# A wide second expert product and a rebuilt router stage in a two-block transformer kernel on one Trainium2 core

## The chip, the core and the metric

The kernel runs on one NeuronCore of one Trainium2 chip. The metric is device microseconds of one execution, taken as the median of several runs. The times of the single instructions come from one further execution under the hardware profiler.

## What is computed

Two transformer blocks run over 2048 tokens of width 1024 in fp32. The first is a hybrid mixer, the second has two kinds of attention and a layer of 32 experts. The change touches the end of the second block: the attention output is projected, added to the residual and normalised (h1); a router picks four experts per token; each expert is a gated MLP; the gated sums are added and normalised again.

```python
h = _layernorm(DEEPNORM_ALPHA_2 * h + mix, ln1_g[i], ln1_b[i])
...
def _moe_sequence(h, w_router, b_router, w_gate_up, b_gate_up, w_down, b_down):
    L = h.shape[0]
    logits = (jnp.einsum('ld,de->le', h, w_router) + b_router).astype(jnp.float32)
    top_val, top_idx = lax.top_k(logits, TOP_K)
    gates = jax.nn.softmax(top_val, axis=-1).astype(h.dtype)
    ...
    hgu = lax.ragged_dot(xs, w_gate_up, group_sizes) + b_gate_up[e_sorted]
    act = _clamped_swiglu(hgu)
    out = lax.ragged_dot(act, w_down, group_sizes) + b_down[e_sorted]
    out = out * gates.reshape(-1)[order][:, None]
    return jax.ops.segment_sum(out, tok, num_segments=L)
```

## The kernel before

Every fp32 product is made of three TensorE products of a high and a low part (`mm3`, lines 72 to 74): a weight or activation is cast on ScalarE to the high part (line 67), and the rest is taken by a subtraction on VectorE or GpSimd (line 68). The engines have their own instruction queues and each works strictly in the order in which the program issues; the program writes that order out by hand.

**The router stage** (`phase_f`, about 2532 to 2824 us) runs over 16 tiles of 128 tokens. `project(n)` multiplies tile n by the output weights: two column halves, eight steps of three products of 512 columns each, and after each half VectorE adds the residual (line 1579). While tile n is projected, a `plan` (lines 1855 to 1862) places the other work of its neighbours at steps 0 to 15: `normed(n-1)` at the start (row statistics, line 1586 and 1588, then a reciprocal square root in two GpSimd instructions, lines 78 and 79), `finished(n-1)` (ScalarE normalises, VectorE multiplies by the gain, GpSimd adds the bias, then SyncE stores h1), the router product and `select(n-2)` (scores, the four best, their exponentials, the one-hot rows `hot` and their sum `mk`), `share` (the gates), `gates` (a dense row of gates), `places` (two small TensorE products of `mk` count the tokens of each expert, VectorE works out each token's slot in its expert's table), four `scatter`s (GpSimd indirect DMAs into four tables), and `bias_t` and `bias` (the experts' output biases, line 1690 transposes the dense gates). After the last projection a tail does what is left: all routing of the last two tiles, the six scatters that were left over and the four of the last tile, the ranking of the experts by load (`ranks`), the last biases and `overflow`. Only then SyncE can read which expert comes first, and the expert stage begins with reading the tables (line 1949) and gathering the token rows (line 1968).

**The expert stage** (`phase_g`, to the end) runs 16 rounds of two experts, A and B, with fixed capacities (`CAPS`). An expert's first product (`up`) has eight items of 256 weight columns, its second (`down`) four. Each item is one 1 MB weight load into `raw` (three buffers) on SyncE, cut into two halves (`split_half`, five buffers of each part) that are made two items ahead (`ensure`). An `up` item makes two PSUM tiles (`pj`, four buffers), which are evicted by `gate`, and one item later `glu` and `keep` write the activation into `at[:, f]` for item f. A `down` item multiplies all eight parts of `at` by 256 columns of the second weights, into a PSUM tile `pd` (two buffers) for each token tile; ScalarE scales it by the gate into `y` (line 2107). In the last round the final sum of all tokens and its normalisation run beside the work (`Finish`); the last expert adds its rows onto the sums, normalises them (`RowNorm`) and stores them by indirect DMA. There an `eager` flag lets the first `down` item of all token tiles run on seven of the eight parts before the eighth is waited for.

Of the kernel before, what the change touches and what calls it, by code (L numbers as in the profile page):

```python
# [20 lines left out]
KD = D // 128  # L21
# [1495 lines left out]
def phase_f(cx, a, op, o, h, h1, acc, tables, out):  # L1517
# [3 lines left out]
    with es, tc.tile_pool(name="fp", bufs=4, space=PSUM) as pj, \  # L1521
# [48 lines left out]
        def project(i):  # L1570
            d = st[i]
            ht = d["ht"]
            for m in range(2):
# [5 lines left out]
                nc.vector.scalar_tensor_tensor(ht[:, ms], ht[:, ms], ALPHA, ps, op0=OP.mult, op1=OP.add)  # L1579

        def normed(i):
            d = st[i]
            ht = d["ht"]
            bs = t_.tile([128, 2, 6], F32, name="bs")
            for m in range(2):
                nc.vector.bn_stats(bs[:, m, :], ht[:, m * 512:(m + 1) * 512])
            mv = t_.tile([128, 4], F32, name="mv")
            nc.vector.bn_aggr(mv[:, 0:2], bs)
            cx.rsqrt(mv[:, 2:3], mv[:, 1:2], LN_EPS, 1)
            nc.vector.tensor_scalar(mv[:, 3:4], mv[:, 0:1], mv[:, 2:3], -1.0, op0=OP.mult, op1=OP.mult)  # L1590
            d["mv"] = mv

        def finished(i):
            d = st[i]
            hn = d["hn"] = t_.tile([128, D], F32, name="hn", bufs=4)
            step = D if i < NT - 1 else 512
# [17 lines left out]
        def select(i):  # L1614
# [11 lines left out]
            nc.scalar.activation(gt, v8[:, :TOPK], AF.Exp, bias=nv, accum_out=gs)  # L1626
            i8 = t_.tile([128, 8], mybir.dt.uint32, name="i8")
# [4 lines left out]
            for k in range(TOPK):  # L1632
                nc.vector.tensor_scalar(hot[:, k, :], iof[:, :NE], idf[:, k:k + 1], None, op0=OP.is_equal)
# [8 lines left out]
        def share(i):  # L1642
            gt, gs = st[i]["gt"], st[i]["gs"]
            nc.vector.reciprocal(gs, gs)
            nc.vector.tensor_scalar(gt, gt, gs, None, op0=OP.mult)

        def gates(i):
            d = st[i]
            gt, hot = d["gt"], d["hot"]
            gm = d["gm"] = t_.tile([128, 3, NE], F32, name="gm")  # L1650
            g1 = t_.tile([128, NE], F32, name="g1")
# [3 lines left out]
            three = [q[:, None, :].to_broadcast([128, 3, NE]) for q in (hot[:, TOPK - 1, :], g1)]  # L1655
            nc.vector.scalar_tensor_tensor(gm, three[0], gt[:, TOPK - 1:TOPK], three[1], op0=OP.mult, op1=OP.add)

        def places(i):
            d = st[i]
            gt, hot = d["gt"], d["hot"]  # L1660
# [5 lines left out]
            nc.vector.tensor_tensor(pos, pos, ebase, OP.add)  # L1666
            nc.vector.tensor_tensor(run, ps[:, NE:2 * NE], run, OP.add)
# [4 lines left out]
            di = t_.tile([128, TOPK], I32, name="di")  # L1672
            nc.vector.tensor_copy(di, dst)
            en = t_.tile([128, TOPK, 2], F32, name="en")
            nc.vector.tensor_copy(en[:, 0, 0:1], ids[:, 0, i:i + 1])
            row = t_.tile([128, TOPK], I32, name="row")
            nc.vector.tensor_scalar(row, di, 127, None, op0=OP.bitwise_and)
            nc.vector.tensor_copy(en[:, :, 1], gt)
            nc.vector.tensor_scalar(en[:, 1:, 0], row[:, 1:], -1.0, ids[:, 1, i:i + 1], op0=OP.mult, op1=OP.add)
            d["di"], d["en"] = di, en  # L1680
# [28 lines left out]
        def ranks(_):  # L1709
            pc = pr.tile([128, 512], F32, name="r")  # L1710
# [810 lines left out]
```

## Time and profile before

| | us |
|---|---|
| median of 3 runs | 5385.56 (5380.69 to 5391.58) |
| the profiled execution | 5383.15 |
| its span, first to last instruction | 5381.2 |

Times in the rows are microseconds from the span's start. A row of a timeline gives start, length, engine, line, operation, the tiles written and read, and in brackets how long the engine had been idle before and what ended that. A TensorE product's length is modelled and overlaps the next one's, so its cost is read from start to start. PEclk is the granted TensorE clock: 1.00 is 2.4 GHz and 0.50 is 1.2 GHz.

### The profile page before, as it was taken

How to read it: one execution, taken by the hardware profiler on the slowest of the kernel's cores; microseconds unless marked ns; L12 is line 12 of the kernel's file. 1: busy time of each engine (PE TensorE's matmuls, PEld its weight loads, DVE VectorE, ACT ScalarE, POOL GpSimd, SP SyncE). 2: the span in 40 equal slices, each digit the busy share in tenths (PEclk: the TensorE clock that was granted, in tenths of full speed). 3: DMA queues.
4: the chain of work that ended last, by engine and by line, in shares of the span. 5: the costliest groups of instructions: out<-in, count | busy, mean ns of one | idle time of the engine just before them, and what ended most of it. 6: DMA issues, size and time to landing. Idle time of an engine off the chain costs nothing. (4 is left out here: it accounts for less than half of the span.)

```text
span 5381.2 us, 89111 instructions
## 1 busy us (share of the span) xinstructions
PE 5179.1 (96%) x33672; PEld 4795.2 (89%) x33672; DVE 3721.3 (69%) x6827; ACT 2690.7 (50%) x5404; POOL 1607.1 (30%) x1571
## 2 busy tenths in 40 slices
PE   8999999899899999999979999999999999999997
PEld 7888878688799999998769999999999999998886
DVE  6787777634688866666887755667767667767758
ACT  4344433333577755555326444545545555556543
POOL 1232226655100021001443233223333333323227
PEclk9999999899999999999989999999999999999998
DMA  4333344344520011011437566556666666767675
GB/s 132 114 106 98 98 143 162 118 125 138 152 67 27 29 52 36 28 36 61 147 103 224 178 182 184 164 163 201 202 195 204 195 202 187 213 188 207 203 212 181
DMA packets 733017, 761.08 MB, mean 141 GB/s; under 512 B 109700, under 2 KB 673870, under 8 KB 732582
## 3 DMA queue, kind: packets, MB, share of 16 engines
q1 hardware_dynamic: 702768, 678.51, 40.3%
q0 software_dynamic: 27776, 74.33, 5.6%
q8 instruction: 267, 4.37, 0.3%
q10 hardware_dynamic: 2038, 2.48, 0.1%
q14 instruction: 168, 1.38, 0.1%
HBM read 626.35 MB, written 128.84 MB: 140 GB/s over the span
## 5 line engine op out<-in xcount | busy, mean ns | idle before, releaser
L68 DVE TENSOR_TENSOR wlo<-raw,whi 128x1024 fp32r<-128x1024 f32 (+1 forms) x751 | 925.8, 1243 | 433.1 <-ACT whi L67 428.5
L67 ACT CAST whi<-raw 128x1024 fp32r<-128x1024 f32 (+1 forms) x1000 | 961.6, 988 | 491.8 <-PE pj L73 176.7
L68 POOL TENSOR_TENSOR wlo<-raw,whi 128x1024 fp32r<-128x1024 f32 (+1 forms) x249 | 553.6, 2223 | 1708.0 <-ACT whi L67 1600.3
L72 PE MATMUL pj<-xsA,whi 128*128 128x256 f32 (+11 forms) x1792 | 595.2, 332 | 20.8 <-DVE g L2048 9.9
L73 PE MATMUL pj<-xsA,whi 128*128 128x256 f32 (+11 forms) x1792 | 592.2, 330 | 0.1
L74 PE MATMUL pj<-xsA,wlo 128*128 128x256 f32 (+11 forms) x1792 | 590.6, 330 | 0.3 <-DVE wlo L68 0.3
L67 ACT CAST ph<-T 128x512 fp32r<-128x512 f32 x512 | 301.0, 588 | 374.8 <-PE T L1349 369.2
L2016 PE MATMUL pj<-xsB,whi 128*128 128x312 f32 (+11 forms) x1664 | 482.2, 360 | 3.9 <-DVE g L2046 3.9
L68 DVE TENSOR_TENSOR pl<-T,ph 128x512 fp32r<-128x512 f32 x512 | 353.4, 691 | 165.5 <-ACT ph L67 156.1
L2018 PE MATMUL pj<-xsB,wlo 128*128 128x156 f32 (+11 forms) x1664 | 417.6, 251 | 0.0
L72 PE MATMUL pd<-whi,atA 128*128 128x256 f32 (+4 forms) x1360 | 395.3, 291 | 17.4 <-ACT atA L67 15.0
L73 PE MATMUL pd<-wlo,atA 128*128 128x256 f32 (+4 forms) x1360 | 384.4, 283 | 8.1 <-POOL wlo L68 7.0
L1330 ACT ACTIVATE P<-S,nm 128x384 f32<-128x384 f32 (+2 forms) x640 | 384.6, 610 | 8.1 <-DVE nm L1324 4.8
L74 PE MATMUL pd<-whi,atA 128*128 128x256 f32 (+4 forms) x1360 | 384.0, 282 | 4.0 <-DVE atA L68 3.9
L72 PEld LDWEIGHTS pj<-xsA,whi 128*128 128x128 f32 x1792 | 341.1, 190 | 35.0 <-ACT g L2043 10.6
L1319 DVE TENSOR_REDUCE mx<-S 128x1 f32<-128x384 f32 (+2 forms) x640 | 355.1, 580 | 24.5 <-PE S L1318 21.5
L74 PEld LDWEIGHTS pj<-xsA,wlo 128*128 128x128 f32 x1792 | 341.4, 191 | 11.3 <-DVE wlo L68 0.5
L73 PEld LDWEIGHTS pj<-xsA,whi 128*128 128x128 f32 x1792 | 341.7, 191 | 9.6 <-DVE xsA L68 0.4
L1334 POOL COPY P<-P 128x48 f32<-128x48 f32 x128 | 28.8, 225 | 1036.1 <-ACT P L1330 1023.3
L2016 PEld LDWEIGHTS pj<-xsB,whi 128*128 128x128 f32 x1664 | 314.3, 189 | 14.6 <-DVE g L2046 4.7
L2018 PEld LDWEIGHTS pj<-xsB,wlo 128*128 128x128 f32 x1664 | 319.1, 192 | 0.2
L72 PE MATMUL pj<-xh,whi 128*128 128x512 f32 (+1 forms) x784 | 314.2, 401 | 3.7 <-ACT whi L67 3.7
(583 smaller groups left out, 14496.1 us busy)
## 6 DMA issues: line engine op xcount, KB each, us to landing
raw<-in_w_gate_up_dram SPq DMA_DIRECT2D x256, 1024.0 KB, 6.3
raw<-in_w_down_dram SPq DMA_DIRECT2D x128, 1024.0 KB, 5.0
raw<-in_w_in_dram SPq DMA_DIRECT2D x120, 512.0 KB, 3.6
ht<-h SPq DMA_DIRECT2D x32, 512.0 KB, 3.7
xt<-in_x_dram SPq DMA_DIRECT2D x30, 512.0 KB, 3.9
hT<-gt SPq DMA_DIRECT2D x20, 512.0 KB, 3.1
hf<-hT SPq DMA_DIRECT2D x40, 256.0 KB, 4.0
h<-xt SPq DMA_DIRECT2D x16, 512.0 KB, 2.7
```

The costliest lines, as they stand in the source:

```text
L67: nc.scalar.copy(hi, src)
L68: (lo_engine or nc.vector).tensor_tensor(lo, src, hi.bitcast(F32), OP.subtract)
L72: mm(ps, w[0], x[0], start=start, stop=False)
L73: mm(ps, w[0], x[1], start=False, stop=False)
L74: mm(ps, w[1], x[0], start=False, stop=stop)
L1319: nc.vector.tensor_reduce(self.mx[j][:, g:g + 1], po, AX.X, OP.max)
L1330: nc.scalar.activation(self.P[j][:, c0:c1], self.sg.pop((j, g)), AF.Exp, bias=self.nm[j], scale=self.scale, accum_out=self.sm[j][:, g:g + 1])
L1334: nc.gpsimd.tensor_copy(meta[:, 1:, :], meta[:, :1, :].to_broadcast([128, 3, N_META]))
L2016: mm(ps[:, :2 * n], hi[:, k, :], self.xp[:, k, :], start=first, stop=False)
L2018: mm(ps[:, :n], lo[:, k, :], xs[:, k, 0, :], start=False, stop=last)
```

## The change

In the router stage VectorE alone normalises: the statistics of each half are taken as soon as the half is there, `finished` is two VectorE instructions of 128x1024 (the second one needs the reciprocal square root), and the ScalarE and GpSimd steps go. The one-hot rows are made by one instruction, the dense gates by one (exponentials of all 32 scores, times the mask, times the reciprocal sum), the running count starts from the experts' base addresses. Under the last projection tile 14 is routed as well, with its four scatters, so that the tail holds tile 15 alone. In the expert stage a `down` item is now 512 columns by half of the contraction: items 0 and 1 make the first 512 columns, 2 and 3 the others, each token tile's PSUM tile stays open over two items, and `close` evicts 512 columns at once. `pj` has six buffers and `pd` is gone; the `eager` order of the last round is gone too.

```diff
                 nc.vector.scalar_tensor_tensor(ht[:, ms], ht[:, ms], ALPHA, ps, op0=OP.mult, op1=OP.add)
+                if m == 0:
+                    d["bs"] = t_.tile([128, 2, 6], F32, name="bs")
+                nc.vector.bn_stats(d["bs"][:, m, :], ht[:, ms])
...
-            nc.vector.tensor_scalar(mv[:, 3:4], mv[:, 0:1], mv[:, 2:3], -1.0, op0=OP.mult, op1=OP.mult)
...
+            nc.vector.scalar_tensor_tensor(hn, d["ht"], mv[:, 0:1], rows["ln1_g_2"], op0=OP.subtract, op1=OP.mult)
...
-                nc.scalar.activation(hn[:, cs], d["ht"][:, cs], AF.Identity, bias=d["mv"][:, 3:4],
-                                     scale=d["mv"][:, 2:3])
-                nc.vector.tensor_tensor(hn[:, cs], hn[:, cs], rows["ln1_g_2"][:, cs], OP.mult)
-                (nc.gpsimd if i < NT - 1 else nc.vector).tensor_tensor(hn[:, cs], hn[:, cs], rows["ln1_b_2"][:, cs],
-                                                                       OP.add)
+                nc.vector.scalar_tensor_tensor(hn[:, cs], hn[:, cs], mv[:, 2:3], rows["ln1_b_2"][:, cs], op0=OP.mult,
+                                               op1=OP.add)
...
+            ex = d["ex"] = t_.tile([128, NE], F32, name="ex")
+            nc.scalar.activation(ex, lg, AF.Exp, bias=nv)
...
-            for k in range(TOPK):
-                nc.vector.tensor_scalar(hot[:, k, :], iof[:, :NE], idf[:, k:k + 1], None, op0=OP.is_equal)
+            nc.vector.tensor_tensor(hot, iof[:, None, :NE].to_broadcast([128, TOPK, NE]),
+                                    idf[:, :, None].to_broadcast([128, TOPK, NE]), OP.is_equal)
...
         def share(i):
-            nc.vector.tensor_scalar(gt, gt, gs, None, op0=OP.mult)
+            en = d["en"] = t_.tile([128, TOPK, 2], F32, name="en")
+            nc.vector.tensor_copy(en[:, 0, 0:1], ids[:, 0, i:i + 1])
+            nc.vector.reciprocal(d["gs"], d["gs"])
+            nc.vector.tensor_scalar(en[:, :, 1], d["gt"], d["gs"], None, op0=OP.mult)
 
         def gates(i):
-            nc.vector.tensor_scalar(g1, hot[:, 0, :], gt[:, 0:1], None, op0=OP.mult)
-            for k in range(1, TOPK - 1):
-                nc.vector.scalar_tensor_tensor(g1, hot[:, k, :], gt[:, k:k + 1], g1, op0=OP.mult, op1=OP.add)
...
+            three = [q[:, None, :].to_broadcast([128, 3, NE]) for q in (d["ex"], d["mk"])]
+            nc.vector.scalar_tensor_tensor(gm, three[0], d["gs"], three[1], op0=OP.mult, op1=OP.mult)
...
                 if n == NT - 1:
-                    plan = [q for q in plan if q[2] is not bias and q[2] is not bias_t]
+                    plan = [(1, n - 2, routed), (1, n - 1, finished), (2, n - 3, scatter, 2), (2, n - 2, select),
+                            (4, n - 2, share), (4, n - 2, gates), (4, n - 3, scatter, 3),
+                            (5, n - 1, transposed, "hn", "x", 0), (6, n - 1, transposed, "hn", "x", 1),
+                            (6, n - 2, places)]
+                    plan += [(7 + k, n - 2, scatter, k) for k in range(TOPK)]
+                    plan += [(9, n - 1, routed), (10, n - 1, select), (10, n - 1, share), (12, n - 1, places)]
+                    plan += [(13 + k // 2, n - 1, scatter, k) for k in range(TOPK)]
...
-            select(i)
             routed(j)
-            share(i)
-            places(i)
-            for k in (2, 3):
-                scatter(i - 1, k)
-            for k in range(TOPK):
-                scatter(i, k)
             select(j)
             share(j)
             places(j)
-            ranks(j)
             for k in range(TOPK):
                 scatter(j, k)
+            ranks(j)
...
-    with es, tc.tile_pool(name="gp", bufs=4, space=PSUM) as pj, \
-            tc.tile_pool(name="gq", bufs=2, space=PSUM) as pq, \
-            tc.tile_pool(name="gr", bufs=2, space=PSUM) as pd:
+    with es, tc.tile_pool(name="gp", bufs=6, space=PSUM) as pj, \
+            tc.tile_pool(name="gq", bufs=2, space=PSUM) as pq:
...
-            def down_src(self, cs):
-                return wdn[bass.ds(self.e, 1), :, cs * 256:(cs + 1) * 256].rearrange("o (k p) m -> p (o k) m", p=128)
+            def down_src(self, i):
+                c, kh = divmod(i, 2)
+                return wdn[bass.ds(self.e, 1), kh * 512:(kh + 1) * 512, c * 512:(c + 1) * 512].rearrange(
+                    "o (k p) m -> p (o k) m", p=128)
...
+                for j in range(self.nt):
+                    if kh == 0:
+                        self.open[j] = pj.tile([128, 512], F32, name="pj")
+                    self.product(self.open[j], j, ws, kh)
+                    if kh == 1:
+                        self.close(self.open.pop(j), j, c, feed)
...
+            def close(self, pt, j, c, feed):
+                y = self.y[j][:m, c * 512:(c + 1) * 512]
+                if self.base is None:
+                    nc.scalar.activation(y, src, AF.Copy, scale=self.gt[:m, j:j + 1])
+                else:
+                    nc.vector.scalar_tensor_tensor(y, src, self.gt[:m, j:j + 1], y, op0=OP.mult, op1=OP.add)
+                    feed.summed(j, c)
...
-                    A.eager = B.eager = True
```

## Rows read from the trace of the kernel before

**Rows 1.** The page's first part: busy us, share, instructions of each engine.
```profile
PE 5179.1 (96%) x33672; PEld 4795.2 (89%) x33672; DVE 3721.3 (69%) x6827; ACT 2690.7 (50%) x5404; POOL 1607.1 (30%) x1571
```
**Rows 2.** Windows: stretch, length, busy PE, PEld, DVE, ACT, POOL, PEclk, DMA.
```profile
2640.00:2680.00 40.00, 37.44 (x210) 30.74 (x210) 35.38 (x103) 14.44 (x33) 18.88 (x23) 1.00 0.39 133
2860.00:2920.00 60.00, 60.00 (x488) 60.00 (x487) 55.84 (x103) 39.49 (x62) 18.39 (x16) 1.00 0.72 229
```
**Rows 3.** Waits of PE, 2600 to 2910: total us, times, longest.
```profile
PE r L1690 <- DVE pos L1665: 14.1, 11, 1.3
```
**Rows 4.** Timeline of DVE over one router tile.
```profile
2642.72 0.21 DVE L1588 BATCH_NORM_AGGREGATE mv<-bs 128x2 f32<-128x12 f32 x1
2643.95 0.21 DVE L1590 TENSOR_SCALAR mv<-mv 128x1 f32<-128x1 f32 x1 [1.02 <-POOL mv L79]
...
2647.53 1.22 DVE L1601 TENSOR_TENSOR hn<-hn,ln_g 128x1024 f32<-128x1024 f32 x1
...
2651.36 0.30 DVE L1652 TENSOR_SCALAR g<-hot,gt 128x32 f32<-128x32 f32 x1
...
2659.67 0.21 DVE L1588 BATCH_NORM_AGGREGATE mv<-bs 128x2 f32<-128x12 f32 x1
```
**Rows 5.** Timeline of POOL in the same tile.
```profile
2648.90 2.40 POOL L1602 TENSOR_TENSOR hn<-hn,ln_b 128x1024 f32<-128x1024 f32 x1 [3.73 <-PE pj L74]
```
**Rows 6.** Line 1645, 2550 to 2790: count, ns min/median/max, first and last start.
```profile
L1645 DVE TENSOR_SCALAR gt<-gt,gs x14: 2401/2460/2465, 2564.5 to 2783.2; 128x4 f32<-128x4 f32 x14
```
**Rows 7.** Timeline after the last projection, DVE and POOL.
```profile
2799.86 0.18 DVE L1618 TENSOR_TENSOR lg<-r,b_router 128x32 f32<-128x32 f32 x1
...
2804.15 0.18 DVE L1618 TENSOR_TENSOR lg<-r,b_router 128x32 f32<-128x32 f32 x1
...
2813.18 0.96 POOL L1684 DMA_INDIRECT table<-en,di  x1 [0.30 <-issue]
2817.54 0.20 POOL L1954 TENSOR_TENSOR tk<-tk 128x8 f32<-128x8 f32 x1 [3.40 <-DMA tk<-table]
```
**Rows 8.** Timeline of PE: two ends of three back-to-back runs of products.
```profile
3089.80 0.28 PE L74 MATMUL pd<-whi,atA 128*128 128x256 f32 x1
...
3092.26 0.28 PE L74 MATMUL pd<-whi,atA 128*128 128x256 f32 x1
...
5291.88 0.40 PE L72 MATMUL pj<-xsA,whi 128*128 128x512 f32 x1
...
5300.05 0.40 PE L74 MATMUL pj<-xsA,wlo 128*128 128x512 f32 x1
...
900.00 0.39 PE L72 MATMUL pj<-wm,hh 128*128 128x512 f32 x1
...
902.95 0.39 PE L73 MATMUL pj<-wm,hh 128*128 128x512 f32 x1
```
**Rows 9.** Waits of PE, 2900 to the end.
```profile
PE pj L2016 <- DVE g L2046: 15.1, 5, 10.7
PE pd L72 <- ACT atA L67: 15.0, 4, 6.1
PE pj L72 <- DVE g L2048: 9.9, 3, 5.0
PE pj L72 <- ACT g L2043: 9.7, 2, 7.1
```
**Rows 10.** Timeline rows of PE and ACT at two of those waits.
```profile
4057.98 0.58 PE L72 MATMUL pd<-whi,atA 128*128 128x256 f32 x1 [4.13 <-ACT atA L67]
...
5021.22 1.11 ACT L67 CAST whi<-raw 128x1024 fp32r<-128x1024 f32 x1 [10.98 <-DMA raw<-in_w_gate_up_dram]
...
5027.68 0.79 PE L2016 MATMUL pj<-xsA,whi 128*128 128x504 f32 x1 [10.68 <-DVE g L2046]
```
**Rows 11.** A window after the second of them, columns as in rows 2.
```profile
5022.00:5032.00 10.00, 4.32 (x13) 3.76 (x14) 8.92 (x14) 6.49 (x13) 2.42 (x1) 0.50 0.72 228
```
**Rows 12.** Timeline of DVE at the very end.
```profile
5368.61 1.28 DVE L2207 SCALAR_TENSOR_TENSOR xg<-y,mv 128x1024 f32<-128x1024 f32 x1
```

More of the change, by code (lines that the diff above doesn't have):

```diff
@@ L1709, in ranks @@
         def ranks(_):
+            total = const([128, NE], F32, "total")
+            nc.vector.tensor_tensor(total, run, ebase, OP.subtract)
             pc = pr.tile([128, 512], F32, name="r")
-            nc.tensor.transpose(pc[:NE, :128], run, cx.ident)
+            nc.tensor.transpose(pc[:NE, :128], total, cx.ident)
             cnt = const([NE, 1], F32, "cnt")
@@ L1942, in __init__ @@
                 self.rest = self.sizes[-1] if self.sizes[-1] <= 64 else 0
-                self.base, self.eager = None, False
+                self.open = {}
+                self.base = None
             def prep(self):
@@ L2074, in keep, with down @@
                                         OP.subtract)
-            def down(self, cs, get, begin, end, feed):
+            def down(self, i, get, begin, end, feed):
+                c, kh = divmod(i, 2)
                 ws = [get(0)]
@@ L2080, in down @@
                 end()
-                if self.base is not None and cs == 2:
-                    self.kept = ws
-                    return
-                todo = [(cs, ws)]
-                if self.base is not None and cs == 3:
-                    todo = [(2, self.kept), *todo]
                 if self.base is not None:
@@ L2114, in product @@
-            def product(self, pt, j, ws, ks):
+                for j in range(self.nt):
[4 more added lines that the diff above has]
+                        self.close(self.open.pop(j), j, c, feed)
+                    if feed is not None:
+                        feed.spread(j, i)
+            def close(self, pt, j, c, feed):
+                m = self.sizes[j]
+                src = ps = pt[:m]
+                if m <= 64:
+                    src = t_.tile([64, 512], F32, name="ys", bufs=1)[:m]
+                    nc.scalar.copy(src, pt[64:64 + m])
+                    nc.vector.tensor_tensor(src, ps, src, OP.add)
+                y = self.y[j][:m, c * 512:(c + 1) * 512]
[4 more added lines that the diff above has]
+                    feed.summed(j, c)
@@ L2115, in product @@
+            def product(self, pt, j, ws, kh):
                 at, m = self.at, self.sizes[j]
                 js = slice(j * 128, j * 128 + m)
-                for k in ks:
-                    wh, wl = [q[:, k % 4, :] for q in ws[k // 4]]
+                for kk in range(4):
+                    k = 4 * kh + kk
+                    wh, wl = [q[:, kk % 2, :] for q in ws[kk // 2]]
                     if m <= 64:
                         both = at[:, k, 0, js.start:js.stop + 64]
-                        mm(pt[:64 + m, :256], both, wh, start=k == 0, stop=False)
-                        mm(pt[:64 + m, :256], both, wl, start=False, stop=k == KD - 1)
+                        mm(pt[:64 + m], both, wh, start=k == 0, stop=False)
+                        mm(pt[:64 + m], both, wl, start=False, stop=k == KD - 1)
@@ L2305, in ensure @@
                     pool = i > 0 and t == 1 and (sl.cls == "A" if kind == "up" else i % 2 == 0)
-                    halves[ready[0]] = split_half(raws[i], t, kind == "up" and not sl.flat,
+                    halves[ready[0]] = split_half(raws[i], t, "flat" if kind == "up" and sl.flat else kind,
                                                   nc.gpsimd if pool else nc.vector)
```

80 lines of the change are left out of this document (22 added, 58 removed).

## The prediction

> **What bounds the kernel now.** I read the page's shares first: TensorE is busy 96% of the span and no other engine over 69% [rows 1]. A share over the whole span hides stages, so the windows come next. In the router stage VectorE is busy 35.4 of 40 us beside TensorE's 37.4; in the expert stage TensorE is busy all 60 of 60 us and VectorE 55.8 [rows 2]. Then the waits of TensorE say who ends last. In the router stage it is VectorE: 14.1 us in 11 waits of `bias_t` [rows 3]. In the expert stage the waits are few and single: evictions of PSUM tiles that came late (15.1, 9.9 and 9.7 us) and late parts of the activation (15.0 us) [rows 9]. So router work is worth time where it shortens VectorE; expert work is worth time where it shortens TensorE's own stream or one of those waits.
>
> **Router loop.** One tile takes 2659.67 - 2642.72 = 16.95 us on VectorE [rows 4]. In it VectorE is held up twice. It waits 1.02 us for GpSimd's reciprocal square root [rows 4]; afterwards that result is wanted only by the second normalising instruction, several us later, so the wait goes. And a multiplication of 4 elements takes 2.40 to 2.47 us in all 14 tiles [rows 6], exactly while GpSimd adds the bias for 2.40 us [rows 5]. I read that as VectorE standing still until GpSimd's add is done; without the add some 0.2 us are left, so 2.2 us go. The Trainium skill says the same ("SBUF — State Buffer", its part on the two sides and the shared port pair): of VectorE and GpSimd, whoever has the shared pair keeps it for the whole instruction and the other one blocks.
>
> Added: two 128x1024 instructions of 1.28 us [rows 12] in place of one of 1.22 [rows 4], so +1.34. Removed: three of four gate instructions (the first takes 0.30 [rows 4], so some 0.8 with the others) and a few tiny ones that I don't count. VectorE's tile becomes 16.95 - 1.02 - 2.2 + 1.34 - 0.8 = 14.3 us. TensorE's tile without its wait of 14.1/11 = 1.28 us is 16.95 - 1.28 = 15.7 us. So **TensorE becomes the bound, with 1.4 us to spare on VectorE**, and what is gained is TensorE's wait: 13 tiles have a `bias_t` under a projection, 13 x 1.28 = **17 us**. If the spare were eaten up (scatters of GpSimd against the new instructions), half of it, 8 us, would be left. ScalarE loses a 128x1024 instruction and gains one of 32 elements; SyncE's h1 store now waits for VectorE instead of GpSimd at the same place. Both lie beside other work.
>
> **Last projection and tail.** Moved under the projection: tile 14's routing. In the tail VectorE spent 2804.15 - 2799.86 = 4.3 us on it before it began with tile 15 [rows 7]. Against that stand two things. TensorE does the router product of tile 14 (16 products narrower than 256 columns; at a 256-wide one's 0.117 us [rows 8] some 1.9 us) inside the projection, which ends later by about that. And GpSimd is passed by four scatters of tile 14, emitted ahead of tile 15's reciprocal square root: 0.96 us and 0.30 between them [rows 7], 5.0 us in all, that can start only when `places(14)` is done, close to the projection's end. The root then comes some 2.5 us later than it could, and the second normalising instruction, the transposes and the router product queue behind it. What that takes away is about what the shorter normalisation gives. Left over is a tail in which tile 15 begins at once, with four scatters behind it instead of eight; the last one starts at 2813.18 and the tables land at 2817.54 now [rows 7], and everything up to the first expert product hangs on that. I take 4.3 - 1.9 + 0.6 (fewer small instructions and a shorter normalisation, less the late root) = **3 us**, between 6 (the root is not late) and -3 (it is late by all 5 us).
>
> By that rule of the Trainium skill on the shared port pair the root can't run under the first normalising instruction of tile 15 either, because that reads two SBUF operands: this would take 1 us off the 3. It speaks against this change, and the place to see it is the wait before the second instruction.
>
> **Wide second product, steady.** From the capacities there are 7072 products of 256 columns; they become 3536 of 512. Start to start, 21 steps of 256 took 2.46 us, 117.1 ns each; 35 steps of 512 in the expert stage's first product took 8.17 us, 233.4 ns; 13 steps of 512 in the first block took 2.95 us, 226.9 ns [rows 8]. A wide one replaces two: 234.2 against 233.4 gives 3536 x 0.8 ns = **3 us**; against 226.9 it gives 26 us. I take the first, the same stage; the other is a rival. By the Trainium skill ("TensorE: Matmul & The Clock Gate", back-to-back issue gap) each product pays about 2.5 ns beside its columns; halving their number would give an estimated 3536 x 2.5 = 9 us instead of 3. The rows of one stage don't show that much, those of the other more.
>
> The weights' bytes, the casts, the halves and the number of items stay. ScalarE evicts 512 columns half as often, beside other work; its latency is covered by the two PSUM buffers that four open token tiles leave.
>
> **Waits of the expert stage.** (a) `down` waits for the last part of the activation because its first token tile runs through all eight parts at once: 15.0 us in four waits, the longest 6.1 in the last round [rows 9], one of 4.13 at 4057.98 [rows 10]. Afterwards item 0 wants only parts 0 to 3, and with three token tiles it lasts 3 x 12 x 0.233 = 8.4 us, where the wait came after 21 products, 21 x 0.117 = 2.5 us: it is covered. In the main rounds this is 15.0 - 6.1 = 9 us. (b) `up` waits for evictions, 15.1 + 9.9 us in eight waits [rows 9]. At 5027.68 the cause is seen: a weight load was late, ScalarE's cast waited 10.98 us for it, and the eviction stands behind that weight's subtraction on VectorE [rows 10]. With six buffers instead of four TensorE can begin as soon as the weight's high part is cast, 5021.22 + 1.11 = 5022.3, 5.3 us sooner. Such waits are due to the load, not the buffers, so I count half: 12 us. (c) After such a wait the clock is at 1.2 GHz: 13 products in 10 us at 0.50 [rows 11]. Some seven waits, 2 us behind each, of which I count a third: 5 us. Sum **26 us**; bounds 5 (VectorE, 55.8 of 60 busy [rows 2], gives the time back) and 42.
>
> **Last round.** The 9.7 us for ScalarE's evictions and the 6.1 for the activation [rows 9] come from a stretch where VectorE also carries the final normalisation; it is late next, so most of it comes back. The last item's token tiles come every 2.8 us instead of two blocks in 5.6, and VectorE has two 1.28 us instructions [rows 12] and three smaller ones for each, some 4 us: the end trails TensorE by about 4 us more. I take **2 us** gained, bounds 9 and -6.
>
> **Sum.** 17 + 3 + 3 + 26 + 2 = 51 us off the profiled execution's 5383.15, which gives 5332; it stands 2.4 below the median (2 lie outside the span), so **5334** for the median.
>
> **Rivals.**
> - *The waits come back* (0.24). Evictions and activation are late because VectorE and the loads are late, and VectorE's 93% in an `up` phase leaves no slack. Then router and tail, 20 us, and 3 us remain: 5362. For it: the load behind 5021.22. Against: `down` phases lie between.
> - *Wide products at the first block's pace* (0.12): 23 us more, 5311. Against: the same stage's 233.4.
> - *It doesn't do what it says* (0.06): the router loop finds another bound within the 1.4 us of spare and the waits come back as well; 5376 to 5396. Against: rows 5 and 6 are the same in all tiles.
> - *Slower* (0.07). A 512-wide second product could cost more than two narrow ones: it reads freshly cast weights while ScalarE and VectorE write the next ones, which no row shows for this width with weights moving. Each ns costs 3.5 us; the other gains are 48, so it decides from 234.2 + 13.6 = 248 ns on. At 252 it is 5399. Against: 233.4 stands in a busy stretch.
>
> **How the numbers follow.** Forecast 0.51, rivals as given. A measurement tells about 0.2%, 11 us, from no change. The forecast, the second rival and nearly all of the first are faster by more: 0.87. Same 0.06, slower 0.07. The range 5290 to 5374 takes in the forecast's bounds, the returned waits and the quick products, and leaves out about 0.15.
>
> **What would show it.** Right: no wait before the transpose of line 1690, a router tile of 15.6 us and line 1645's multiplication at 0.2 us; the four `atA` waits gone; wide products at 233 ns. Wrong: wide products off 233 ns by more than 5; PE waiting on `xg` or weights where it waited on evictions; tile 15's second normalising instruction waiting over 3 us on POOL; an end that trails TensorE by over 20 us.

## The result: 5321.6 us, a ratio of 0.988

| | before | after |
|---|---|---|
| median | 5387.55 (5380.69 to 5391.58, 4 runs) | 5321.61 (5318.40 to 5324.02, 4 runs) |
| span of the profiled execution | 5381.2 | 5318.5 |

The ratio of after to before is 0.9879, with a 95% interval from 0.9861 to 0.9896: 56 to 75 us off 5387.55. The forecast was 51 off, 5334. So the sign and the order of size came out, and the gain was larger than the sum said. Where it lies is read from five marks in the two traces: the starts of the first and the last product of the projections, of the first `up` product, of the last `down` product of the last expert B (what is called the main rounds ends there, so they are 15 rounds and expert B of the sixteenth), and the end of the span. The last round below is thus the last expert A alone.

| stretch | before | after | difference | forecast |
|---|---|---|---|---|
| router loop: first to last projection product | 265.8 | 250.5 | -15.4 | -17 + 1.9 |
| tail: to the first `up` product | 41.5 | 37.1 | -4.4 | -3 - 1.9 |
| main rounds: to the last product of the last expert B | 2367.0 | 2320.6 | -46.4 | -29 |
| last round (the last expert A): to the end of the span | 183.7 | 186.1 | +2.4 | -2 |

The loop and the tail came out as forecast, 19.7 against 20 together. Most of the error is in the main rounds.

### The profile page after: what moved, and what is told of

Read it like the earlier page. It is cut to its first block, busy times and chain, and to the rows that moved or that the text cites. A ratio compares the mean times of both kernels' runs of the same rounds, so it can differ in the third digit from the quotient of the medians.

```text
span 5318.5 us, 81631 instructions
## 1 busy us (share of the span) xinstructions
PE 5158.1 (97%) x30136; PEld 4583.9 (86%) x30136; DVE 3687.1 (69%) x6664; ACT 2635.8 (50%) x5229; POOL 1586.3 (30%) x1556
## 5 line engine op out<-in xcount | busy, mean ns | idle before, releaser
L1349 PE MATMUL T<-ident,P 128*128 128x128 f32 x2048 | 307.5, 273 | 4.1 <-DVE pl L68 2.4
L74 PE MATMUL pj<-xh,wlo 128*128 128x512 f32 (+1 forms) x784 | 307.4, 392 | 3.1 <-POOL wlo L68 3.1
L73 PE MATMUL pj<-xl,whi 128*128 128x512 f32 (+1 forms) x784 | 306.8, 391 | 0.0
```

Of the source, the lines that this page charges most:

```text
L73: mm(ps, w[0], x[1], start=False, stop=False)
L74: mm(ps, w[1], x[0], start=False, stop=stop)
L1349: nc.tensor.transpose(ps[:, i, j * 128:(j + 1) * 128], self.P[j][:, k0:k0 + 128], cx.ident)
```

## The profile after

The page's first part, and two windows (columns as in [rows 2]), one in the router stage and one in the first round:

```profile
PE 5158.1 (97%) x30136; PEld 4583.9 (86%) x30136; DVE 3687.1 (69%) x6664; ACT 2635.8 (50%) x5229; POOL 1586.3 (30%) x1556
```
```profile
2640.00:2680.00 40.00, 40.00 (x217) 32.71 (x216) 33.95 (x87) 14.47 (x37) 19.56 (x24) 1.00 0.38 132
2842.00:2902.00 60.00, 60.00 (x487) 60.00 (x487) 55.30 (x104) 38.74 (x60) 17.45 (x16) 1.00 0.69 229
```

In the router stage TensorE is now busy 40.00 of 40 us and VectorE 33.95; before it was 37.44 and 35.38 [rows 2]. TensorE has become the bound, as the prediction said. The timeline of VectorE over one tile (columns as in [rows 4]):

```profile
2621.22 0.21 DVE L1587 BATCH_NORM_AGGREGATE mv<-bs 128x2 f32<-128x12 f32 x1
2621.62 0.19 DVE L1615 TENSOR_TENSOR lg<-r,b_router 128x32 f32<-128x32 f32 x1 [0.19 <-PE r L1609]
...
2624.61 0.69 DVE L68 TENSOR_TENSOR ol<-tr,oh 128x512 fp32r<-128x512 f32 x1 [0.32 <-ACT oh L67]
2625.22 1.27 DVE L1595 SCALAR_TENSOR_TENSOR hn<-ht,mv,ln_g 128x1024 f32<-128x1024 f32 x1
2626.61 1.28 DVE L1599 SCALAR_TENSOR_TENSOR hn<-hn,mv,ln_b 128x1024 f32<-128x1024 f32 x1
...
2628.06 0.23 DVE L1646 TENSOR_SCALAR en<-gt,gs 128x4 f32<-128x4 f32 x1
...
2632.30 0.69 DVE L68 TENSOR_TENSOR xl<-tr,xh 128x512 fp32r<-128x512 f32 x1 [0.61 <-issue]
2633.43 0.69 DVE L68 TENSOR_TENSOR xl<-tr,xh 128x512 fp32r<-128x512 f32 x1 [0.44 <-ACT xh L67]
...
2636.67 0.21 DVE L1587 BATCH_NORM_AGGREGATE mv<-bs 128x2 f32<-128x12 f32 x1
```

A tile takes 2636.67 - 2621.22 = 15.45 us instead of 16.95 [rows 4]. The multiplication of four elements takes 0.23 us instead of 2.46 [rows 6], and it is VectorE now that waits, 1.56 us in these four rows, for TensorE and ScalarE where a releaser is named.

From 2830 to 5100 us, which are the main rounds without their two ends, the longest waits of TensorE are these (columns as in [rows 9]):

```profile
PE tr L1969 <- DVE xsA L68: 5.6, 3, 2.3
PE pj L2008 <- ACT whi L67: 5.5, 1, 5.5
PE tr L1969 <- DVE xsB L68: 4.4, 2, 2.4
PE tr L1969 <- DMA xg<-h,tok: 2.5, 2, 2.3
```

The evictions (15.1 and 9.9 us) and the main rounds' share of `atA` (9) of [rows 9] are gone; a late weight and the transposes of gathered rows are what is left. In the last expert A, from 5135 us on, a wait for the activation has stayed (6.4 us; before, the longest was 6.1):

```profile
PE pj L72 <- ACT atA L67: 6.4, 1, 6.4
PE pj L73 <- POOL wlo L68: 5.9, 1, 5.9
```

At the end, three timelines: the last product's start on TensorE before, the same in after, then VectorE's last instructions in after.

```profile
5366.68 0.28 PE L74 MATMUL pd<-whi,atA 128*128 128x256 f32 x1
```
```profile
5296.83 0.39 PE L74 MATMUL pj<-whi,atA 128*128 128x512 f32 x1
```
```profile
5291.83 0.74 DVE L2098 SCALAR_TENSOR_TENSOR y<-pj,gt,y 128x512 f32<-128x512 f32 x1
...
5296.06 0.75 DVE L2098 SCALAR_TENSOR_TENSOR y<-pj,gt,y 128x512 f32<-128x512 f32 x1
5297.94 1.28 DVE L2200 SCALAR_TENSOR_TENSOR atB<-atB,rs,y 128x1024 f32<-128x1024 f32 x1 [1.14 <-POOL rs L79]
...
5301.31 0.75 DVE L2098 SCALAR_TENSOR_TENSOR y<-pj,gt,y 128x512 f32<-128x512 f32 x1
...
5308.48 1.28 DVE L2200 SCALAR_TENSOR_TENSOR xg<-xg,rs,y 128x1024 f32<-128x1024 f32 x1 [1.84 <-POOL rs L79]
```

VectorE needs 5.25 us for a token tile (5296.06 to 5301.31), while TensorE closes one every 12 x 0.233 = 2.8 us. The span ends 5318.5 - 5296.8 = 21.7 us after the last product's start; before it was 14.5.

## The experiments

Each set of runs has its own runs of the kernel before; the ratio and its 95% interval are against those. Equal code repeats well in the main rounds: six profiles with the expert code of after (the last round differs in some) gave 2316.3 to 2321.2 us, three with that of before 2357.9 to 2367.0.

### The two stages apart

The first kernel has `phase_f` of after and `phase_g` of before, the second the reverse. As diffs against the kernel before they are the hunks of the change in the one function:

```diff
 def phase_f(...):
...
-                (nc.gpsimd if i < NT - 1 else nc.vector).tensor_tensor(hn[:, cs], hn[:, cs], rows["ln1_b_2"][:, cs],
-                                                                       OP.add)
...
```


> The router stage of the changed kernel with the expert stage of the kernel before. Theory (the two stages add up): the first up product comes 19.7 us sooner as in the changed kernel, the expert stage lasts as before, so 20 us less in all, about 5367. Rival (an earlier start of the expert stage is given back there, since loads and VectorE are what is late): the expert stage's waits of TensorE grow by 10 us or more and the time is 5375 to 5385.

```diff
 def phase_g(...):
...
-    with es, tc.tile_pool(name="gp", bufs=4, space=PSUM) as pj, \
+    with es, tc.tile_pool(name="gp", bufs=6, space=PSUM) as pj, \
...
```


> The router stage of the kernel before with the expert stage of the changed one. Theory: last product of the main rounds 46 us after what it was relative to the first up product less, last round 2 us longer, so 44 us less, about 5343; together with the router part it gives the 66 us of the whole change. Rival: the two parts need each other, and the sum of the two alone is over 75 or under 55 us.

Measured: router alone 5364.78 us against 5381.50, ratio 0.9967 (0.9955 to 0.9980); expert stage alone 5341.08, ratio 0.9923 (0.9906 to 0.9939). The main rounds behind the new router last 2366.0 us, as before; the new main rounds behind the old router 2321.2. 0.33% and 0.77% make 1.1%, the whole change 1.21%: within their intervals the stages add up, and the trace shows nothing of the earlier start given back.

### The bias add on VectorE, one line of the router stage

```diff
-                (nc.gpsimd if i < NT - 1 else nc.vector).tensor_tensor(hn[:, cs], hn[:, cs], rows["ln1_b_2"][:, cs],
-                                                                       OP.add)
+                nc.vector.tensor_tensor(hn[:, cs], hn[:, cs], rows["ln1_b_2"][:, cs],
+                                                                       OP.add)
```


> The kernel before with one edit in the router stage: the bias add of the normalisation goes from GpSimd to VectorE in all tiles. Theory (VectorE's 2.46 us multiplication of four elements stands still for GpSimd's add): that multiplication falls to about 0.2 us, VectorE's tile is 16.95 + 1.22 - 2.2 = 16.0 us, the first up product comes 12 to 14 us sooner, about 5369. Rival (the multiplication is slow for another reason, and the add is only put on top): tile 18.2 us, 16 us longer, about 5398.

Measured: 5364.59 against 5388.78, ratio 0.9961 (0.9947 to 0.9975); the loop lasts 252.8 us instead of 265.8. The timeline of VectorE, with two starts of the same instruction:

```profile
2643.12 1.23 DVE L1602 TENSOR_TENSOR hn<-hn,ln_b 128x1024 f32<-128x1024 f32 x1
...
2644.46 0.23 DVE L1645 TENSOR_SCALAR gt<-gt,gs 128x4 f32<-128x4 f32 x1
...
2659.04 1.23 DVE L1602 TENSOR_TENSOR hn<-hn,ln_b 128x1024 f32<-128x1024 f32 x1
```

The tile is 15.92 us, against 16.0 expected, and the small multiplication 0.23: although VectorE does 1.23 us more work a tile, it is done 1.03 us sooner. So it had stood still for GpSimd's add, and this one line brings 13.0 us in the loop, 11.5 up to the first `up` product. (By the ratio it is 21 us in all. The main rounds of this profile last 2357.9 us, those of the two others with the same expert code 2366.0 and 2367.0; that these 8 us come from the edit is not shown.)

### Tile 14 back in the tail

With the routing of tile 14 the ranking, too, goes back to its old place, ahead of tile 15's scatters.

```diff
-                    plan = [(1, n - 2, routed), (1, n - 1, finished), (2, n - 3, scatter, 2), (2, n - 2, select),
...
-                    plan += [(13 + k // 2, n - 1, scatter, k) for k in range(TOPK)]
+                    plan = [q for q in plan if q[2] is not bias and q[2] is not bias_t]
...
             normed(j)
+            routed(i)
             finished(j)
...
```


> The changed kernel with tile 14's routing back in the tail behind the last projection, in the order of the kernel before; new instructions kept. Theory (the move is worth 3 us): last projection product 1.9 us sooner after the start of the stage, first up product 3 to 6 us later, 5325 to 5328. Rival (the root queued behind four scatters takes the gain): first up product within 1 us of the changed kernel's, 5321.

Measured: 5318.28 against 5388.78, ratio 0.9874 (0.9857 to 0.9890), not to be told from the changed kernel's 0.9879. The loop lasts 246.7 us and the tail 40.6, together 287.2; in after 250.5 and 37.1, together 287.6. The move shortens the tail by 3.4 us and lengthens the projection by 3.8: it is worth nothing. The first `up` product comes 0.4 us sooner than in the changed kernel, so the rival's number holds; where the gain went is the longer projection as well as the root. The loop without it gains 265.8 - 246.7 = 19.1 us.

### The buffers alone, the early parts alone, both

```diff
-    with es, tc.tile_pool(name="gp", bufs=4, space=PSUM) as pj, \
-            tc.tile_pool(name="gq", bufs=2, space=PSUM) as pq, \
-            tc.tile_pool(name="gr", bufs=2, space=PSUM) as pd:
+    with es, tc.tile_pool(name="gp", bufs=6, space=PSUM) as pj, \
+            tc.tile_pool(name="gq", bufs=2, space=PSUM) as pq:
...
-                    pt = open_[j] if early else pd.tile([128, 512], F32, name="pd")
+                    pt = open_[j] if early else pj.tile([128, 512], F32, name="pj")
```


> The kernel before with its four and two PSUM buffers of the expert stage made one ring of six; products stay 256 wide and in the old order. Theory (step b of the prediction: the buffers remove the waits of up for evictions): PE's waits on g (15.1 and 9.9 us) fall to under 5, the low clock behind them goes too, 20 to 25 us less, about 5363; the waits for atA stay at some 9 us in the main rounds. Rival (the waits belong to the loads and to VectorE, or the down items now take the buffers that up wants): the waits come under other names, less than 8 us gained, 5377 to 5390.

```diff
-                self.base, self.eager = None, False
+                self.base, self.eager = None, True
```


> The kernel before, in which each expert's first item of the second product runs through parts 0 to 6 of all its token tiles before part 7, as only the last round did; all products still 256 wide, buffers as before. Theory (step a: atA waits go when the item's first product does not want the last part at once): the atA waits of the main rounds, 9 us, fall to under 1 and some clock with them, 9 to 13 us less, about 5375. Rival (the wait moves to the next one in line, evictions of the two pd buffers or of pj, which the opened tiles now take): under 4 us gained, 5383 to 5395.

Measured: the buffers alone 5381.36 us, ratio 1.000 (0.9991 to 1.001); the early parts alone 5379.67, ratio 0.9998 (0.9987 to 1.0008). Neither does anything to the time, within some 5 us. TensorE's waits show why (these lists go from 2870 to 5195 us, from behind the first gathers); first with six buffers, then with early parts:

```profile
PE pj L72 <- ACT atA L67: 18.5, 5, 4.1
PE pj L2015 <- ACT whi L67: 5.7, 1, 5.7
PE pj L72 <- ACT atA L2069: 4.4, 2, 2.8
PE tr L1978 <- DMA xg<-h,tok: 3.2, 1, 3.2
```
```profile
PE pj L2016 <- DVE g L2046: 14.9, 4, 10.3
PE pj L72 <- DVE g L2048: 7.4, 3, 4.5
PE tr L1979 <- DVE xsA L68: 5.1, 10, 1.5
PE tr L1979 <- DMA xg<-h,tok: 4.8, 2, 3.8
PE pd L72 <- ACT y L2107: 4.5, 12, 1.2
PE pj L72 <- ACT whi L67: 3.0, 2, 2.8
```

With six buffers the waits for evictions of `g` are gone, 25.0 us in [rows 9], and those for `atA` have grown from 9.8 to 22.9: TensorE runs ahead to the `down` item, and there the same late chain of ScalarE and VectorE still has the activation to write. With early parts the `atA` waits are gone and the evictions stay, with new small waits for `y` and `xsA`. Then both edits together:

```diff
-    with es, tc.tile_pool(name="gp", bufs=4, space=PSUM) as pj, \
+    with es, tc.tile_pool(name="gp", bufs=6, space=PSUM) as pj, \
...
-                self.base, self.eager = None, False
+                self.base, self.eager = None, True
```


> The kernel before with both single edits together: one ring of six PSUM buffers and, for every expert, parts 0 to 6 of all token tiles ahead of part 7. Products stay 256 wide and the loads as they were. Theory now (a late chain of ScalarE and VectorE hits the next thing that TensorE needs of it, up's buffers or the activation; only cover at both places removes it): g and atA waits both under 5 us, main rounds 25 to 36 us shorter, about 5350. Rival (the width of the product, or its weights loaded as half of the inner dimension, does it): the waits come under further names as in the single edits, less than 8 us gained, 5374 to 5385.

Measured: 5361.26 against 5382.32, ratio 0.9957 (0.9943 to 0.9971). Two edits of which each is worth nothing are worth 21 us together, and the main rounds are 20.5 us shorter. Waits:

```profile
PE tr L1978 <- DVE xsA L68: 7.5, 13, 1.7
PE pj L2015 <- ACT whi L67: 6.3, 1, 6.3
PE tr L1978 <- DMA xg<-h,tok: 5.0, 2, 3.8
PE pj L72 <- ACT atA L67: 3.2, 3, 1.2
```

It is less than the 25 expected at least: some short waits are left, and the changed kernel is another 26 us ahead in the main rounds.

### The width alone

The order, loads and buffers of the changed kernel, with its wide products (those of the token tiles over 64 rows) issued as pairs:

```diff
-                        cx.mm3(pt[:m], (at[:, k, 0, js], at[:, k, 1, js]), (wh, wl), k == 0, k == KD - 1)
+                        for c in range(2):
+                            cs = slice(c * 256, c * 256 + 256)
+                            cx.mm3(pt[:m, cs], (at[:, k, 0, js], at[:, k, 1, js]), (wh[:, cs], wl[:, cs]),
+                                   k == 0 and c == 0, k == KD - 1 and c == 1)
```


> The changed kernel with each 512-wide second product issued as two of 256 columns into the two halves of the same bank; loads, items, buffers and order stay. Theory now (from the difference of all second products between the kernel with six buffers and early parts and the changed one, 808.3 against 795.7 us in the main rounds, a wide product saves 3.2 ns on the mean, though the medians say 0; and narrow products let some waits come back): 11 us from the products and up to 10 from waits, 5330 to 5343. Rival (the prediction's 0.8 ns from the medians and no more): 5324.

Measured: 5328.67 against 5388.78, ratio 0.9893 (0.9876 to 0.9909). It is some 7 us above the changed kernel's 0.9879, though the two intervals overlap; the trace is sharper: main rounds 2328.5 us, 7.9 longer. The waits hardly change (28.7 against 27.4 us in the table below), so the part of the theory by which narrow products bring waits back is not borne out; the products themselves come out between the theory's 11 us and the rival's 3.

The main rounds of these kernels, worked out from the starts of all of TensorE's products: time from start to start less the waits (over 50 ns) is put down to the first product of each step. "Low" is the time of products begun at the 1.2 GHz clock, which lies in the other columns. The names are those of the expectations; eager is the flag of the kernel before.

```
kernel        main rounds   waits   up products   down products   other   low
before          2367.0       49.4      1449.6          810.1       57.8   46.1
six_buffers     2363.6       45.8      1441.5          816.7       59.6   48.5
eager_all       2364.9       49.2      1449.3          807.6       58.8   35.7
six_eager       2346.5       37.7      1440.8          808.3       59.7   24.2
two_halves_b    2328.5       28.7      1440.8          801.2       57.7   20.2
after           2320.6       27.4      1440.1          795.7       57.4   19.3
pj_five         2324.7       28.3      1443.6          795.5       57.3   23.8
```

The waits can be checked in the windows of the main rounds: 2366.0 - 2316.4 = 49.6 us without a product before, 2320.0 - 2292.6 = 27.4 after.

```profile
2831.00:5197.00 2366.00, 2316.40 (x16747) 2267.32 (x16747) 1617.90 (x2481) 1266.44 (x2006) 729.81 (x468) 0.99 0.66 194
```
```profile
2812.00:5132.00 2320.00, 2292.63 (x13406) 2060.48 (x13407) 1612.65 (x2455) 1226.93 (x1832) 727.14 (x468) 0.99 0.67 198
```

Wide products save 801.2 - 795.7 = 5.5 us in place of 2928 pairs, 1.9 ns each, at the same low clock (20.2 and 19.3 us). In the other profiles with the expert code of after this column reads 793.6 to 797.3 us, and less half of its own low time 793.0 to 794.1, against 799.6 for the pairs: 1.9 to 2.3 ns. The waits and the low time spread more over equal code: 44.6 to 49.7 and 37 to 47 us in the three profiles with the expert code of before, 25.0 to 27.4 and 15 to 24 in the six with that of after.

### Five buffers in the changed kernel

```diff
-    with es, tc.tile_pool(name="gp", bufs=6, space=PSUM) as pj, \
+    with es, tc.tile_pool(name="gp", bufs=5, space=PSUM) as pj, \
```


> The changed kernel with five PSUM buffers in the ring instead of six, all else as it is. Theory: with four open token tiles one buffer is left for what follows, so TensorE waits again for evictions, at the change from one expert's second product to the next one's first: 8 to 25 us longer, 5330 to 5347, waits on y and g. Rival (the wide order alone covers it, six were not needed): under 4 us, 5318 to 5326.

Measured: 5324.66 against 5382.32, ratio 0.9887 (0.9866 to 0.9908). The theory missed; the time lies in the rival's range, and evictions stay off the list of waits but for one of 0.5 us. The main rounds are 4.1 us longer than in after, and 3.5 to 8.4 longer than in the six profiles of its expert code, so the sixth buffer may be worth a few microseconds; the times don't resolve it.

### The end

```diff
+                if self.base is not None and i == 2:
+                    self.kept = ws
+                    return
                 for j in range(self.nt):
+                    if self.base is not None and i == 3:
+                        self.open[j] = pj.tile([128, 512], F32, name="pj")
+                        self.product(self.open[j], j, self.kept, 0)
                     if kh == 0:
```


> The changed kernel, but in the last expert the halves of item 2 are kept and items 2 and 3 run together for each token tile (both halves of the inner dimension, then the eviction), as the kernel before did. Theory (the end is late because token tiles close every 2.8 us and VectorE and GpSimd take some 5 us for each): tiles close every 5.6 us, the end trails the last product by 14 to 16 us instead of 21.7, 5 to 7 us less, about 5315. Rival (TensorE waits instead, because item 2 no longer starts while item 3's weights are cast): the last product comes 4 us later and under 3 us are gained.

Measured: 5316.78 against 5382.32, ratio 0.9880 (0.9863 to 0.9896). The time shows nothing of it. The trace does: the last round is 181.0 us instead of 186.1, and the span ends 15.7 us after the last product's start instead of 21.7. VectorE, in the timeline, now waits for TensorE before each tile:

```profile
5285.80 0.75 DVE L2104 SCALAR_TENSOR_TENSOR y<-pj,gt,y 128x512 f32<-128x512 f32 x1 [1.49 <-PE pj L74]
...
5291.40 0.75 DVE L2104 SCALAR_TENSOR_TENSOR y<-pj,gt,y 128x512 f32<-128x512 f32 x1 [1.48 <-PE pj L74]
...
5296.28 1.28 DVE L2206 SCALAR_TENSOR_TENSOR xg<-xg,rs,y 128x1024 f32<-128x1024 f32 x1 [0.77 <-POOL rs L79]
```

A last kernel was to move the scatters of tile 14 behind tile 15's root as well, beside the edit above. Its first form took out another line than meant: tile 13's four scatters were left out, and tile 14's were issued both ahead of the root and behind it.

```diff
-                    plan += [(7 + k, n - 2, scatter, k) for k in range(TOPK)]
...
             normed(j)
+            for k in range(TOPK):
+                scatter(i, k)
             finished(j)
```


> The changed kernel with two edits: the last expert's items 2 and 3 together for each token tile (as in the run before), and tile 14's four scatters issued behind tile 15's reciprocal square root instead of ahead of it. Theory: VectorE's wait of 1.84 us for the root in the tail is gone and the first up product comes 1.5 to 2 us sooner after the last projection, the end trails the last product by 15 to 16 us, together 6 to 8 us less than the changed kernel, about 5314. Rival (the scatters come late now and hold up tile 15's own): first up product no sooner, 5316 to 5318.

Measured: 5316.34 against 5388.78, ratio 0.9868 (0.9851 to 0.9884). It says nothing on the root, which still ran behind four scatters; the trail at the end is 15.7 us again. The second form:

```diff
-                    plan += [(13 + k // 2, n - 1, scatter, k) for k in range(TOPK)]
...
             normed(j)
+            for k in range(TOPK):
+                scatter(i, k)
             finished(j)
```


> The changed kernel with the last expert's items 2 and 3 together for each token tile, and tile 14's four scatters issued behind tile 15's reciprocal square root instead of ahead of it. In the changed kernel the root's input is ready at 2776.78, its two instructions run at 2779.02 and 2779.34 right behind the scatters, and VectorE waits 1.84 us for them. Theory 1 (only the queue held the root): it runs beside the first normalising instruction, VectorE's wait is 0, 1.8 us gained. Theory 2 (that instruction, 1.28 us long, holds GpSimd off as well, as the prediction's sentence on the shared port pair has it): the root starts when it ends, VectorE still waits 0.9 us, 0.9 us gained. Theory 3 (the scatters, now behind the root, hold up the tables): first up product later by 1 us or more. With either of the first two and an end that trails by 15.7 us, 6 to 8 us less than the changed kernel, about 5314.

Measured: 5321.29 against 5384.92, ratio 0.9884 (0.9868 to 0.9901). In the tail of after, the timelines of GpSimd and then VectorE read:

```profile
2778.03 0.96 POOL L1675 DMA_INDIRECT table<-en,di  x1 [0.30 <-issue]
2779.02 0.24 POOL L78 TENSOR_SCALAR mv<-mv 128x1 f32<-128x1 f32 x1
```
```profile
2776.81 1.28 DVE L1595 SCALAR_TENSOR_TENSOR hn<-ht,mv,ln_g 128x1024 f32<-128x1024 f32 x1
2779.94 0.75 DVE L1599 SCALAR_TENSOR_TENSOR hn<-hn,mv,ln_b 128x512 f32<-128x512 f32 x1 [1.84 <-POOL mv L79]
```

and with the root ahead of the scatters:

```profile
2781.79 1.32 POOL L78 TENSOR_SCALAR mv<-mv 128x1 f32<-128x1 f32 x1 [2.95 <-DVE mv L1587]
```
```profile
2781.74 1.28 DVE L1595 SCALAR_TENSOR_TENSOR hn<-ht,mv,ln_g 128x1024 f32<-128x1024 f32 x1
2783.79 0.75 DVE L1599 SCALAR_TENSOR_TENSOR hn<-hn,mv,ln_b 128x512 f32<-128x512 f32 x1 [0.78 <-POOL mv L79]
```

The second theory holds: the root's first instruction takes 1.32 us instead of 0.24, as long as VectorE's instruction beside it lasts, and VectorE's wait falls from 1.84 to 0.78 only. And the third theory's sign came as well: the first `up` product is not sooner but 39.8 us behind the last projection instead of 37.1, because the tables' reads and the gather behind the scatters took longer (TensorE waits 8.55 us for the first gathered rows instead of 3.57). The last scatter itself starts sooner, 18.4 us behind the last projection instead of 19.6, so it is not, as that theory had it, the scatters that came late. What made the reads longer stays open: six kernels with the tail of before show 41.5 to 43.6 us for that stretch, but the five with the unchanged tail of after show 37.1 to 37.2. None of the variants beats the changed kernel by more than its measurement tells.

## Why the prediction was right, and where its sum was wrong

**Router loop, 17.** Right, mechanism and size. The wait for the root and the 2.2 us standstill went, TensorE became the bound, and its tile came out at 15.45 us where 15.7 was worked out. The one-line run shows that the standstill on GpSimd's add is the larger part (13.0 us); the rest, 19.1 - 13.0 = 6 us, is all the other edits of the loop together. That loop and tail together meet the forecast is luck in part: without the move of tile 14 the loop gained 19.1 us, not 17, and the tail 1.0, and the move, priced at 3 in the next term, added nothing.

**Tail, 3.** Mis-sized, by the step that costs the routing of tile 14 inside the projection. It gave 1.9 us; undoing the move showed 3.8 against 3.4 us gained in the tail. The router product of tile 14 takes 2768.19 to 2769.89, 1.7 us, as worked out; two waits of TensorE in that projection, 0.47 us for `lg` and 0.44 for `en`, neither of which is there with the move undone, were not counted, and the last 1.2 us are not traced. The late root was there as described: it cost 1.84 us of VectorE's time, of the 2.5 estimated. By the Trainium skill ("SBUF — State Buffer", its part on the two sides) the root could not run under the first normalising instruction; the 1.32 us of the last run agree: of the 1.84 us, 1.06 were the queue's and 0.78 belong to that instruction, where the prediction's sentence had 1.

**Wide products, 3.** Mis-sized. The step that failed is taking one quiet run of 21 products for the pitch of the narrow ones: its 234.2 ns for a pair against 233.4 gave 0.8 ns. The run with the width undone gives 1.9 ns for a pair, which makes 3536 x 1.9 = 6.7 us. The sentence on the Trainium skill's 2.5 ns per product ("TensorE: Matmul & The Clock Gate", back-to-back issue gap), 9 us, is nearer to that than the rows were. The slow rival, over 248 ns, and the quick one, 226.9, did not come: 16 steps of 512 in the last item (5285.40 to 5289.14 us, start to start) take 233.8 ns.

**Waits of the expert stage, 26.** Right in what would go, wrong in how it was added up. Terms (a) and (b), 21 us of waits: waits fell from 49.4 to 27.4, by 22 (17 to 25 over the profiles of equal code). All of the evictions of `g` and of the waits for the activation went, 25.0 and 9.8 us, and some 13 us of others came (a late weight, 5.5; transposes for `xsA`, 5.6); counting half of (b) for the load's sake, 12 us, came out near this sum, in part by luck: only the late weight is a load's. Term (c), 5 us of clock: the time at 1.2 GHz fell from 46.1 to 19.3 us. A 256-wide `down` product takes 213 ns there and 117 at full clock (medians in before), so 45% of that time is lost, and some 12 us came back (6 to 15 over the profiles of equal code). The prediction counted seven waits and a third of 2 us behind each; that is the step that failed, and its size is 7 us. Together with the products, 22.0 + 12.1, and 3.1 and 9.2 for what is left of the `up` and `down` columns at full clock, this is the 46.4 us of the main rounds.

But (a) and (b) are no terms of a sum. The runs with one edit each show 0 us for the buffers (the prediction had 12 and took the cause to be solved once TensorE could begin) and 0 for the activation (9); only both bring 21. The likeliest case was right because the change makes both. The first rival, the waits coming back under another name, is just what happens to either edit alone. By how much the half items (four weights' parts at a time over 512 columns, and one eviction instead of two) beat early parts at 256 columns can be seen, 18.0 us between six_eager and two_halves_b, 9.0 of it in waits; 7.1 us lie in second products of the same width. Some 1.5 of these are clock, and some 2 to 3 go with the order of the early parts itself: less half of the low time, the `down` column is 805.0 and 805.3 us with early parts and 802.2 to 803.0 without, at the same width. The rest stays open.

**Last round, 2 gained.** The wrong sign: 2.4 lost. TensorE's part was 4.8 us shorter (its last product starts 164.4 us after the main rounds instead of 169.2), as its waits there fell from 27.1 to 19.2 us: ScalarE's evictions went, the wait for the activation did not. The end trails by 7.2 us more where 4 were worked out. The step that failed is the 4 us for VectorE's work on a token tile: the instructions make 0.75 + 1.28 + 0.69 + 0.21 + 1.28 = 4.2 us, but a wait of 1.1 to 1.8 us for GpSimd's root comes on top in each but the first, since the root queues behind the indirect stores of the tile before. The sign it named for being wrong, a trail of over 20 us, is in the trace: 21.7.

## What to carry to other kernels

Where an engine is late now and then, ask what is next in line to wait for it before counting a buffer as a gain: here two covers were worth nothing each and 21 us together, so add or undo them in pairs. A tiny instruction that takes 2.46 us in one place and 0.23 in another points at a standstill, and moving the work that runs beside it can win even where it goes onto the engine that stood still. Take the pitch of a product from all its steps in a stage, not from one quiet run, and price every wait that goes together with the slow clock behind it.

## What the runs showed of the hardware that was not expected

GpSimd's instructions stretch where they begin inside one of VectorE's normalising instructions: the first step of a root from 0.24 to 1.32 us, and an indirect store at the end of after from 0.96 to 2.08. It is so for every root of after's router stage: 13 first steps of a root begin inside one, take 1.28 to 1.32 us and end 0.08 to 0.09 us behind it, and the 15 others take 0.22 to 0.24. Two of them on GpSimd (the second beside VectorE's row at 2626.61, shown above):

```profile
2621.52 0.23 POOL L78 TENSOR_SCALAR mv<-mv 128x1 f32<-128x1 f32 x1 [4.89 <-DVE mv L1587]
...
2626.66 1.31 POOL L78 TENSOR_SCALAR rs<-rs 128x2 f32<-128x2 f32 x1
```

The six indirect stores of the end that begin inside one end 0.83 to 0.99 us behind it, about the whole length of one that begins elsewhere. In after, VectorE's second normalising instruction starts as soon as the root is done, and GpSimd's store of the same tile starts right inside it, as in this timeline of GpSimd (VectorE's began at 5297.94, shown above):

```profile
5297.33 0.58 POOL L79 TENSOR_TENSOR rs<-rs,mhalf 128x1 f32<-128x1 f32 x1
5298.09 2.08 POOL L2118 DMA_INDIRECT acc<-y,tok  x1 [0.18 <-issue]
5300.47 1.76 POOL L2118 DMA_INDIRECT out_dram<-atB,tok  x1 [0.30 <-issue]
```

With the token tiles further apart (the run of the section on the end), the store that begins before VectorE's instruction (5286.34 against 5286.47) takes 1.07. And the slow clock weighs more than single waits suggest: 22 us of waits removed gave back some 12 us of clock, about half of their own length again.
